# One pair ahead, one product later: reordering projections, splits and output weights in a two-block transformer kernel

## The chip, the cores and the metric
The kernel runs on one core of a Trainium2 chip. The metric is the device time of one execution in microseconds; the time before is the median of three runs.

## The reference
Two blocks of two layers each act on 256 latent tokens x and 256 context tokens (D = 1024, float32). Every layer adds a modulated mixer and a modulated squared-ReLU MLP to the residual.

```
mod   = silu(c) @ w_mod + b_mod                  # 6 x 1024 per layer and stream
a     = rms_norm(h) * g * (1 + scale) + shift
block 1 (l = 0, 1):  p, u, vs, q, k, v, gates = split(a @ w_in)
   attn  = softmax(rope(q) rope(k)^T / 8 + rpb, and q k_ctx^T) @ (v, v_ctx)      # 8 heads of 64
   y     = sig(g0)*(pool(p) @ w_po) + sig(g1)*(sgu(u, vs) @ w_so) + sig(g2)*(attn @ w_ao)
   h    += g1 * (y @ w_o);   h += g2 * (relu(a2 @ w_ff1)**2 @ w_ff2)
block 2, first layer:  mLSTM in chunks, both directions; out = rms(h) * sigmoid(o) @ w_out
block 2, second layer: sliding-window attention, 16 q heads, 4 k/v heads, window 128, a sink per head
```
In l=1 of block 1 and in the last layer the context stream is needed only for k and v.

## The kernel before
Activations stand with features on the 128 partitions and tokens along the free axis: 512 columns, context first (columns 0 to 255), then latent. A float32 product is made of three fast ones: each weight tile is split into a high half whi (ACT) and a low half wlo (VectorE, or GpSimd where `wlow` says so), each activation into xh and xl, and TensorE runs wh·xh, wh·xl and wl·xh for each of 8 k tiles. One output tile of 512 columns is thus 24 matmuls in one PSUM bank. Weights come by DMA into 3 `raw` slots, 512 KB each, and there are 3 slots each for whi and wlo. Products rotate over three PSUM banks (mm, mm, mx); scores have 2 banks (S), transposes 2 (T), outputs of the attention and small sums 1 (acc).

`gemm` takes a list of weights, loads each (`wload`), runs its matmuls (`group`) and calls an `evac` function that empties the bank. An evac may return a further part; it is kept in `late` and run by `flush` after the matmuls of the next product. `head=3` runs the first three tiles side by side, interleaved by k tile with a skew of 2; `tail=3` does the last three stream by stream while the next norm is made. `ready` is a list of weights that are loaded before their product is called; `gemm` and `gemm_rows` take weights from it before they load their own. `drip` issues pieces of the modulation products of later layers (`mod_units`: VectorE, ACT and GpSimd multiply and add, then `mod_out` transposes) at a rate for each stage. `rope` is a permutation matmul on TensorE, a multiplication on GpSimd and a multiplication and addition on VectorE; `put_q` and `put_k` split into halves for two heads. A scheduler orders the instructions of each engine ahead of time, by program order with a bonus for evacuations (`sooner`); at run time each engine works through its own list.

In block 1 (`block1`, run for l = 0 and 1) come the k products, the v product by token rows (`gemm_rows`), all four q products, then four pairs of heads of attention, then the gates and the branch products (`evac_a` adds the branches and splits them into `ys`), then the output product over wo. In the mLSTM `gates_out` runs eight gate products, after which the merged heads are split into ys for mwout. In the sliding-window layer (SWA) q is projected one pair of heads ahead already.

Of the kernel before, what the change touches and what calls it, by code (L numbers as in the profile page):

```python
# [62 lines left out]
class Builder:  # L63
# [140 lines left out]
    def gemm(self, aps, xs, c0, evac, head=0, tail=0, order=(LAT, CTX), pre=None, mid=None, flush=True):  # L204
# [7 lines left out]
        while i < n - tail:  # L212
            m = max(head, 1) if i == 0 else 1
            cols = by_stream if m > 1 and not self.ready else [(c0, T)]
            tiles = [(i + j, self.ready.pop(0) if self.ready else self.wload(aps[i + j], kt))
                     for j in range(m)]
# [7 lines left out]
            if m == 1:  # L224
                self.drip()
# [201 lines left out]
    def mod_units(self, i, groups):  # L427
# [5 lines left out]
        def unit(cg, half, k):  # L433
# [47 lines left out]
    def need(self, i, cg):  # L481
# [314 lines left out]
def block1(b, ph, l, xs, pre, after):  # L796
# [209 lines left out]
def block2_mlstm(b, ph, xs, pre, after):  # L1006
# [115 lines left out]
    def project(hf):  # L1122
# [124 lines left out]
    go = gates_out()  # L1247
    ys = b.new_xs("A")
    for hd in range(8):
        pt = b.ps("S")  # L1250
        for c in range(4):
            b.tr(pt[:, c * P:(c + 1) * P], hs[hd // 4][c][:, hd % 4, :])
        t = b.t("E")
        b.stt(t, go[hd], 1.0, pt, ALU.add, ALU.mult)
        b.act(ys[hd][0], t, scale=hn[:, hd:hd + 1])
        b.stt(ys[hd][1], t, hn[:, hd:hd + 1], ys[hd][0].bitcast(F32), ALU.mult, ALU.subtract)
# [9 lines left out]
def block2_swa(b, ph, xs, pre):  # L1266
# [12 lines left out]
    def evac_k(j, ps, a, e):  # L1279
        if a < L:  # L1280
            b.put_k(kh[2 * j:2 * j + 2], kl[j], slice(0, L), ps[:, :L - a])
        if e > L:
            t, k = b.T1(), b.T1()
            b.act(t, ps[:, max(L - a, 0):])

            def rest():
# [251 lines left out]
```

## Time and profile before
| what | value |
|---|---|
| median of 3 runs | 2288.17 us (2285.65 to 2294.4) |
| profiled execution | 2289.41 us |
| its span, first to last instruction | 2287.6 us |
| TensorE busy | 2184.0 us, 95% |
| VectorE, ACT, GpSimd busy | 1623.2, 1147.6, 703.2 us |
| mean granted clock of TensorE | 0.983 |

Times in the rows below are microseconds from the start of the span, durations too unless marked ns. PEclk is the granted clock as a share of 2.4 GHz. A stretch at 0.5 runs at 1.2 GHz, and its matmuls count as busy. Idle time of an engine stands in brackets in a row of the timeline, with the instruction that ended it.

### The profile page before, as it was taken

Reading aid. Unit: us, or ns where it says so; the run is one execution under the profiler, and the core shown is the slowest. Engines: PE = TensorE matmul, PEld = TensorE weight load, DVE = VectorE, ACT = ScalarE, POOL = GpSimd, SP = SyncE. Lnnn points to the kernel's source line nnn. Section 1 sums busy time; section 2 is a strip of 40 time slices with the busy share of each in tenths; the row PEclk is TensorE's granted clock in tenths of the full one; section 3 lists DMA queues with packets and bytes.
Section 4 is the critical chain, followed back from the end, with each engine's and each line's share of the span. In section 5 each row is a group of like instructions: output and inputs, shape, how many; then the busy total and the mean of one; then the engine's idle time right before and its main releaser. Section 6 shows DMA issues by size and latency. Waiting matters only on the chain.

```text
span 2287.6 us, 36316 instructions
## 1 busy us (share of the span) xinstructions
PE 2184.0 (95%) x13402; PEld 1851.8 (81%) x13402; DVE 1623.2 (71%) x2762; ACT 1147.6 (50%) x2122; POOL 703.2 (31%) x566
## 2 busy tenths in 40 slices
PE   6999999999999999998999899999999999898998
PEld 3777777887777787898899877778777778878998
DVE  4877656687666875778877766778876566698766
ACT  3556434454443455655545646655443433675453
POOL 2640435424221543045300524253432222423001
PEclk9999999999999999999999999999999999999999
DMA  7451445446555443367554323344555532214552
GB/s 276 133 159 59 156 130 180 138 130 187 187 188 167 146 147 107 122 206 219 184 185 158 105 80 102 115 155 130 166 190 179 170 120 74 74 47 147 190 186 96
DMA packets 128146, 336.79 MB, mean 147 GB/s; under 512 B 14944, under 2 KB 24160, under 8 KB 127968
## 3 DMA queue, kind: packets, MB, share of 16 engines
q1 hardware_dynamic: 127968, 334.46, 45.1%
q8 instruction: 106, 1.74, 0.3%
q14 instruction: 72, 0.59, 0.1%
HBM read 333.36 MB, written 1.05 MB: 146 GB/s over the span
## 4 chain that ended last, share of the span: by engine, by line
PE 44%; DVE 7%; issue 3%; ACT 2%; POOL 1%; DMA 1%; DVEq 0%; POOLq 0%; ACTq 0%; SPq 0%
PE mm L122 27%; PE mx L122 11%; PE S L122 2%; DVE wlo L130 1%; PE pv L122 1%; PE T L122 1%; PE T L126 1%; PE num L122 1%; DVE macc L119 1%; ACT whi L116 1%; DMA mraw<-wmod_in 1%; DVE A L119 1%; POOL macc L449 1%; DVE T L119 0%; POOL sums L509 0%
## 5 line engine op out<-in xcount | busy, mean ns | idle before, releaser
L122 PE MATMUL mm<-A,whi 128*128 128x256 f32 (+1 forms) x2600 | 664.6, 343 | 17.7 <-ACT A L116 7.7
L449 POOL TENSOR_TENSOR macc<-macc,mraw 128x512 f32<-128x512 f32 x244 | 364.3, 1493 | 668.9 <-ACT mraw L116 659.9
L122 PEld LDWEIGHTS mm<-A,whi 128*128 128x128 f32 x2600 | 447.4, 191 | 86.2 <-issue 15.2
L122 PE MATMUL mm<-B,whi 128*128 128x256 f32 (+1 forms) x1884 | 457.8, 333 | 6.9 <-DVE B L119 3.8
L122 PE MATMUL mm<-A,wlo 128*128 128x256 f32 (+1 forms) x1300 | 442.0, 340 | 2.6 <-DVE wlo L130 2.6
L130 DVE TENSOR_TENSOR wlo<-raw,whi 128x1024 fp32r<-128x1024 f32 x252 | 345.3, 1372 | 135.3 <-ACT whi L116 133.9
L116 ACT ACTIVATE whi<-raw 128x1024 fp32r<-128x1024 f32 x273 | 287.6, 1056 | 274.5 <-PE mm L122 167.2
L122 PEld LDWEIGHTS mm<-B,whi 128*128 128x128 f32 x1884 | 320.7, 191 | 47.3 <-DVE B L119 4.3
L116 ACT ACTIVATE mraw<-mraw,silu 128x512 f32<-128x512 f32 x244 | 175.3, 722 | 294.5 <-DVE macc L119 180.2
L122 PE MATMUL mx<-A,whi 128*128 128x512 f32 (+1 forms) x1256 | 320.0, 342 | 1.6 <-ACT G L116 1.1
L122 PE MATMUL mm<-B,wlo 128*128 128x256 f32 (+1 forms) x942 | 312.0, 332 | 2.9 <-DVE wlo L130 1.6
L119 DVE SCALAR_TENSOR_TENSOR macc<-mraw,silu,macc 128x512 f32<-128x512 f32 x244 | 258.8, 1061 | 54.9 <-DMA mraw<-wmod_in 52.5
L122 PEld LDWEIGHTS mm<-A,wlo 128*128 128x128 f32 x1300 | 248.6, 191 | 30.3 <-DVE wlo L130 3.0
L116 ACT ACTIVATE whi<-Y 128x1024 fp32r<-128x1024 f32 x152 | 160.7, 1057 | 218.3 <-PE mm L122 154.1
L130 DVE TENSOR_TENSOR wlo<-Y,whi 128x1024 fp32r<-128x1024 f32 x148 | 192.2, 1298 | 90.7 <-ACT whi L116 90.6
L122 PEld LDWEIGHTS mx<-A,whi 128*128 128x128 f32 x1256 | 216.0, 190 | 31.1 <-issue 1.3
L122 PE MATMUL mx<-A,wlo 128*128 128x512 f32 (+1 forms) x628 | 214.9, 342 | 0.3 <-DVE wlo L130 0.3
L122 PE MATMUL mx<-B,whi 128*128 128x256 f32 (+1 forms) x836 | 201.2, 329 | 6.0 <-ACT B L116 3.1
L122 PEld LDWEIGHTS mm<-B,wlo 128*128 128x128 f32 x942 | 179.8, 191 | 21.6 <-DVE wlo L130 1.8
L509 POOL TENSOR_TENSOR sums<-sums,T 128x256 f32<-128x256 f32 x84 | 91.2, 1095 | 298.7 <-ACT T L116 297.2
L119 DVE SCALAR_TENSOR_TENSOR h<-mm,mod,h 128x256 f32<-128x256 f32 x278 | 125.8, 478 | 70.6 <-PE mm L122 70.4
L122 PEld LDWEIGHTS mx<-B,whi 128*128 128x128 f32 x836 | 141.1, 191 | 23.0 <-ACT B L116 3.8
(316 smaller groups left out, 3071.3 us busy)
## 6 DMA issues: line engine op xcount, KB each, us to landing
mraw<-wmod_in SPq DMA_DIRECT2D x352, 256.0 KB, 2.9
Y<-ff_in SPq DMA_DIRECT2D x152, 512.0 KB, 3.7
raw<-ff_in SPq DMA_DIRECT2D x104, 512.0 KB, 3.5
raw<-win_in SPq DMA_DIRECT2D x68, 512.0 KB, 3.8
raw<-mwin_in SPq DMA_DIRECT2D x17, 512.0 KB, 3.5
raw<-wo_in SPq DMA_DIRECT2D x16, 512.0 KB, 4.1
raw<-swin_in SPq DMA_DIRECT2D x10, 512.0 KB, 3.5
B<-wfirst_in SPq DMA_DIRECT2D x16, 256.0 KB, 5.4
```

What stands on the lines that cost most here:

```text
L116: return self.nc.scalar.activation(out, in_, func, **kw)
L119: return self.nc.vector.scalar_tensor_tensor(out, a, scalar, b, op0, op1)
L122: return self.nc.tensor.matmul(out, lhsT=lhsT, rhs=rhs, start=start, stop=stop, **kw)
L126: return self.nc.tensor.transpose(out, in_, self.ident[:k, :k])
L130: (eng or self.nc.vector).tensor_sub(lo, src, hi.bitcast(F32))
L449: self.nc.gpsimd.tensor_add(a1, a1, raw)
L509: (adder or self.nc.gpsimd).tensor_add(sums, sums, sq)
```

## The change
q of block 1 is projected one pair ahead of its attention instead of four pairs at once; its rope and splits, those of k and those of the SWA's q and k become deferred parts, after one copy of the bank; mod_out's transposes are deferred by one more flush; evac_a adds on VectorE for the last two tiles; the last product in front of wo or mwout makes two output weights ready, and the output product begins with three tiles side by side over all columns; `drip` is called once for each tile of a head; gates_out merges and splits each head behind the next gate product; the banks of two `gemm_rows` change their order.

```diff
-    def gemm(self, aps, xs, c0, evac, head=0, tail=0, order=(LAT, CTX), pre=None, mid=None, flush=True):
+    def gemm(self, aps, xs, c0, evac, head=0, tail=0, order=(LAT, CTX), pre=None, mid=None, flush=True,
+             ahead=(), streams=True):
...
-            cols = by_stream if m > 1 and not self.ready else [(c0, T)]
+            cols = by_stream if streams and m > 1 and not self.ready else [(c0, T)]
             tiles = [(i + j, self.ready.pop(0) if self.ready else self.wload(aps[i + j], kt))
                      for j in range(m)]
+            if i + m == n:
+                self.ready = [self.wload(ap, KT) for ap in ahead]
...
-            if m == 1:
+            for _ in range(m):
                 self.drip()
...
-            self.late.append(self.mod_out(i, (cg,), 4 * half, ps))
+            columns = self.mod_out(i, (cg,), 4 * half, ps)
+            self.late.append(lambda: self.late.append(columns))
...
     def evac_k(j, ps, a, e):
-        t = b.T1()
-        b.act(t, ps[:, L:])
-        b.put_k(kh[j], kl[j], slice(0, L), ps[:, :L])
+        t = b.t("E")
+        b.act(t, ps)
         def rest():
             k = b.T1()
-            b.rope(k, t, b.perm1, b.rope1)
+            b.rope(k, t[:, L:], b.perm1, b.rope1)
+            b.put_k(kh[j], kl[j], slice(0, L), t[:, :L])
             b.put_k(kh[j], kl[j], slice(L, T), k)
         return rest
     def evac_q(j, ps, a, e):
-        q, t, k = b.t("Y", (P, 2, T), F32R), b.T1(), b.T1()
-        b.act(t, ps[:, L - a:], scale=0.125)
-        if c0 == 0:
-            b.put_q(q, slice(0, L), ps[:, :L], 0.125)
-        b.rope(k, t, b.perm1, b.rope1)
-        b.put_q(q, slice(L, T), k)
+        q, t = b.t("Y", (P, 2, T), F32R), b.t("W")
+        b.act(t[:, a:], ps, scale=0.125)
         qs.append(q)
+        def rest():
+            k = b.T1()
+            b.rope(k, t[:, L:], b.perm1, b.rope1)
+            if c0 == 0:
+                b.put_q(q, slice(0, L), t[:, :L])
+            b.put_q(q, slice(L, T), k)
+        return rest
...
-    b.gemm([win[6 + j] for j in range(4)], xs, c0, evac_q)
+    def project(j):
+        b.gemm([win[6 + j]], xs, c0, evac_q, flush=False)
+    project(0)
     for j in range(4):
+        if j < 3:
+            project(j + 1)
...
             b.weigh(o, qt, pts, vt, vcols)
+            b.flush()
...
-            nc.gpsimd.tensor_add(t, t, y[d][:, c0:])
+            (nc.vector if d > 5 else nc.gpsimd).tensor_add(t, t, y[d][:, c0:])
...
-        b.gemm2([io[f"wao{l}"][d2]], at, c0, evac_a)
+        b.gemm2([io[f"wao{l}"][d2]], at, c0, evac_a,
+                ahead=[io[f"wo{l}"][d] for d in range(2)] if d2 == 3 else ())
...
-        b.gemm(aps, ys, c0, b.add_to_h(g1), tail=3, mid=b.norm(xs, LAT, A, S))
+        b.gemm(aps, ys, c0, b.add_to_h(g1), head=3, streams=False, tail=3,
+               mid=b.norm(xs, LAT, A, S))
...
-        b.gemm_rows([io["mwv"][hf, j] for j in range(4)], T, xs, ("mm", "mm", "S", "S"),
+        b.gemm_rows([io["mwv"][hf, j] for j in range(4)], T, xs, ("S", "S", "mm", "mm"),
...
-    def gates_out():
-        go = [b.t("B") for _ in range(8)]
-        b.gemm([win[16 + j] for j in range(8)], xs, 0,
-               lambda j, ps, a, e: b.act(go[j][:, a:e], ps, AF.Tanh, scale=0.5))
-        return go
+    def gates_out(hs):
+        ys = b.new_xs("A")
+        def evac(hd, ps, a, e):
+            go = b.t("B")
+            b.act(go, ps, AF.Tanh, scale=0.5)
+            def rest():
...
+            return rest
+        b.gemm([win[16 + j] for j in range(8)], xs, 0, evac,
+               ahead=[io["mwout"][d] for d in range(2)])
+        return ys
...
-    def query(ps):
-        t, q = b.T1(), b.T1()
+    def query(_, ps, a, e):
+        t, out = b.T1(), b.t("Q", (P, 2, L), F32R)
         b.act(t, ps, scale=0.125)
-        b.rope(q, t, perm2, rope2)
-        out = b.t("Q", (P, 2, L), F32R)
-        b.put_q(out, slice(0, L), q)
-        return out
+        qs.append(out)
+        def rest():
+            q = b.T1()
+            b.rope(q, t, perm2, rope2)
+            b.put_q(out, slice(0, L), q)
+        return rest
-    b.gemm_rows([io["swv"][j] for j in range(2)], L, xs, ("mm", "mm", "mx", "S"),
+    b.gemm_rows([io["swv"][j] for j in range(2)], L, xs, ("S", "S", "mm", "mm"),
```

In the instruction lists, the numbers behind a name tell one buffer from another, and what an instruction waits for stands in brackets. First TensorE at the start of the output product of l=0, before: B_632 and B_633 are the halves of the last tile of ys, whi_734 the first wo weight.
```order
L122 MATMUL mx_736_3513<-B_630_2948,whi_734_3509 128x512 [waits Activation_49]
L122 MATMUL mx_736_3513<-B_631_2949,whi_734_3509 128x512 [waits DVE_49]
L122 MATMUL mx_736_3513<-B_630_2948,wlo_735_3510 128x512
L122 MATMUL mx_736_3513<-B_632_2950,whi_734_3509 128x512 [waits Activation_49]
L122 MATMUL mx_736_3513<-B_633_2951,whi_734_3509 128x512 [waits DVE_49]
```
These are the 19th to 23rd of the first tile's 24 matmuls. The same place after, where mm_743 and mm_744 are the second and third tile:
```order
L122 MATMUL mm_743_3526<-B_626_2944,whi_717_3451 128x512
L122 MATMUL mm_743_3526<-B_627_2945,whi_717_3451 128x512
L122 MATMUL mm_743_3526<-B_626_2944,wlo_718_3452 128x512
L122 MATMUL mm_744_3527<-B_622_2940,whi_740_3521 128x512
L122 MATMUL mm_744_3527<-B_623_2941,whi_740_3521 128x512
L122 MATMUL mm_744_3527<-B_622_2940,wlo_741_3522 128x512
L122 MATMUL mx_742_3525<-B_632_2950,whi_714_3445 128x512 [waits Activation_49]
```
The last split is read behind parts of two other tiles: 45 matmuls of the output product stand ahead of it instead of 21.

Second, TensorE in l=1 of block 1 at the products over wvs1 (tiles S), before:
```order
L122 MATMUL mm_1504_7538<-A_1424_7210,whi_1483_7476 128x256
L122 MATMUL mm_1504_7538<-A_1423_7209,wlo_1484_7477 128x256
L122 MATMUL S_1505_7566<-whi_1486_7482,A_1409_7195 128x256 [waits Activation_49]
L122 MATMUL S_1505_7566<-wlo_1487_7483,A_1409_7195 128x256 [waits DVE_49]
L122 MATMUL S_1505_7566<-whi_1486_7482,A_1410_7196 128x256
```
and after, where whi_1517 and wlo_1518 are halves of a further load of wvs1, and mx_1541 is the first k product:
```order
L122 MATMUL mm_1513_7581<-A_1433_7253,whi_1492_7519 128x256
L122 MATMUL mm_1513_7581<-A_1432_7252,wlo_1493_7520 128x256
L122 MATMUL S_1514_7609<-whi_1517_7613,A_1418_7238 128x256 [waits Activation_49]
L122 MATMUL S_1515_7610<-whi_1517_7613,A_1418_7238 128x256
L122 MATMUL mx_1541_7703<-A_1418_7238,whi_1539_7699 128x512 [waits Activation_49]
L122 MATMUL mx_1541_7703<-A_1419_7239,whi_1539_7699 128x512 [waits DVE_49]
L122 MATMUL S_1514_7609<-wlo_1518_7614,A_1418_7238 128x256 [waits DVE_49]
```
Before, the low half wlo_1487 is made on VectorE ahead of the operations T1 and A of the norm; after, wlo_1518 stands behind these:
```order
L130 TENSOR_TENSOR wlo_1496_7526<-raw_1494_7523,whi_1495_7525 128x1024 [waits DMAHW0_49,PE_49,Activation_49]
L130 TENSOR_TENSOR wlo_1499_7532<-raw_1497_7529,whi_1498_7531 128x1024 [waits DMAHW1_49,PE_49,Activation_49]
L119 SCALAR_TENSOR_TENSOR T1_1505_7549<-h_82,A1_0_7236,T1_1504_7547 128x256 [waits Activation_49]
L119 SCALAR_TENSOR_TENSOR T1_1506_7553<-h_82,A1_0_7236,T1_1504_7547 128x256 [waits Pool_49]
...
L119 SCALAR_TENSOR_TENSOR T1_1512_7577<-h_82,A1_0_7236,T1_1504_7547 128x256
L130 TENSOR_TENSOR wlo_1518_7614<-raw_1516_7611,whi_1517_7613 128x1024 [waits DMAHW3_49]
```
No product reads wlo_1496 and wlo_1499, the first pair of low halves of wvs1; between the rows of T1 stand four more of them and five that write A.

Third, VectorE in the SWA attention, before, from the low halves of the next pair's q (Q_3797) to the reduction of its scores (S_3838):
```order
L119 SCALAR_TENSOR_TENSOR Q_3797_19465<-T1_3793_19456,Q_3797_19465 64x256 [waits Activation_49] x2
L130 TENSOR_TENSOR A_3762_19320<-pv_3763_19321,A_3761_19319 128x256 [waits Activation_49]
L748 TENSOR_TENSOR sm_3809_19498<-sm_3809_19498 128x1 [waits Activation_49]
L743 TENSOR_SCALAR sm_3815_19529<-sm_3815_19529,sink_3688_18894 128x1 [waits DVE_49]
L749 RECIPROCAL sm_3809_19498<-sm_3809_19498 128x1 [waits DVE_49]
...
L750 TENSOR_SCALAR E_3817_19534<-E_3817_19534,sm_3816_19530 128x512 [waits DVE_49,PE_49]
L737 TENSOR_REDUCE sm_3840_19630<-S_3838_19624 128x1 [waits PE_49]
```
and after, for the pair with Q_3764 and S_3805 (T_3781 is its permuted q):
```order
L701 TENSOR_TENSOR T1_3783_19380<-T_3781_19377,rope2_3691_18900 128x256 [waits PE_49]
L757 RECIPROCAL sm_3787_19395<-sm_3787_19395 128x1 [waits DVE_49]
L702 TENSOR_TENSOR T1_3780_19376<-T1_3782_19379,T1_3783_19380 128x256 [waits DVE_49,Pool_49]
L758 TENSOR_SCALAR E_3788_19399<-E_3788_19399,sm_3787_19395 128x512 [waits DVE_49]
L119 SCALAR_TENSOR_TENSOR Q_3764_19321<-T1_3780_19376,Q_3764_19321 64x256 [waits Activation_49] x2
L756 TENSOR_TENSOR sm_3792_19413<-sm_3792_19413 128x1 [waits Activation_49]
L757 RECIPROCAL sm_3792_19413<-sm_3792_19413 128x1 [waits DVE_49]
L758 TENSOR_SCALAR E_3793_19417<-E_3793_19417,sm_3792_19413 128x512 [waits DVE_49]
L745 TENSOR_REDUCE sm_3807_19483<-S_3805_19477 128x1 [waits PE_49]
```
Twelve operations stood between the two before, three stand there now.

## Rows read from the trace of the kernel before

**Rows 1.** Head of the page: busy us (share of span) xinstructions
```profile
span 2287.6 us, 36316 instructions
...
PE 2184.0 (95%) x13402; PEld 1851.8 (81%) x13402; DVE 1623.2 (71%) x2762; ACT 1147.6 (50%) x2122; POOL 703.2 (31%) x566
```
**Rows 2.** Table by stretch: us, busy by engine, PEclk, DMA share, GB/s
```profile
100.00:116.00 16.00, 14.00 (x74) 10.43 (x73) 13.23 (x23) 12.73 (x28) 9.06 (x6) 1.00 0.38 122
147.00:165.00 18.00, 15.62 (x60) 11.95 (x59) 16.17 (x23) 9.59 (x18) 10.38 (x7) 0.91 0.52 171
395.00:412.00 17.00, 13.86 (x47) 10.47 (x46) 8.67 (x11) 6.74 (x11) 6.57 (x5) 0.80 0.46 140
842.00:860.00 18.00, 15.34 (x77) 12.63 (x77) 17.03 (x33) 9.73 (x18) 8.46 (x11) 0.91 0.65 221
880.00:892.00 12.00, 7.87 (x28) 5.73 (x27) 6.94 (x12) 7.39 (x16) 1.29 (x1) 0.86 0.17 49
1323.00:1340.00 17.00, 14.16 (x53) 10.70 (x52) 9.68 (x22) 6.85 (x11) 0.00 (x0) 0.90 0.32 104
1500.00:1520.00 20.00, 17.91 (x90) 13.59 (x89) 18.53 (x27) 11.29 (x17) 7.75 (x6) 1.00 0.38 123
1952.00:1965.00 13.00, 11.60 (x96) 11.25 (x95) 4.42 (x9) 9.68 (x22) 4.75 (x2) 1.00 0.23 78
1971.00:1985.00 14.00, 10.14 (x59) 8.79 (x58) 9.18 (x23) 7.28 (x17) 7.67 (x6) 0.88 0.31 104
1985.00:2070.00 85.00, 81.74 (x641) 66.67 (x641) 74.28 (x251) 61.56 (x154) 18.27 (x11) 1.00 0.18 57
...
1559.00:1580.00 21.00, 19.69 (x163) 18.78 (x155) 20.78 (x40) 13.18 (x30) 5.84 (x5) 1.00 0.27 89
```
**Rows 3.** Timeline of PE, 395 to 413: start, us, what, [idle before <-releaser]
```profile
400.80 1.52 PE L122 MATMUL mx<-B,whi 128*128 128x512 f32 x2 [3.14 <-ACT B L116]
...
410.22 0.62 PE L122 MATMUL mm<-B,whi 128*128 128x512 f32 x2
```
**Rows 4.** Timeline of POOL, 385 to 402
```profile
393.19 1.73 POOL L986 TENSOR_TENSOR G<-G,Y 128x512 f32<-128x512 f32 x1 [1.23 <-DVE G L119]
...
397.84 2.24 POOL L986 TENSOR_TENSOR G<-G,Y 128x512 f32<-128x512 f32 x1
```
**Rows 5.** Timeline of DVE, 832 to 853
```profile
840.92 3.33 DVE L119 SCALAR_TENSOR_TENSOR T<-h,A,T 128x256 f32<-128x256 f32 x3
...
849.38 1.22 DVE L130 TENSOR_TENSOR wlo<-raw,whi 128x1024 fp32r<-128x1024 f32 x1
```
**Rows 6.** Timeline of PE, 876 to 895
```profile
885.35 0.76 PE L122 MATMUL mx<-whi,A 128*128 128x512 f32 x1 [3.24 <-DVE B L719]
```
**Rows 7.** Timeline of ACT, 1324 to 1331
```profile
1327.16 0.63 ACT L116 ACTIVATE nM<-W 64x512 fp32r<-64x512 f32 x1 [2.90 <-DVE W L1068]
1327.70 0.57 ACT L116 ACTIVATE Q<-mm 128x512 f32<-128x512 f32 x1
```
**Rows 8.** Timeline of PE, 838 to 856
```profile
850.49 0.50 PE L122 MATMUL mm<-A,whi 128*128 128x512 f32 x1 [1.58 <-ACT whi L116]
```
**Rows 9.** Timeline of DVE, 1990 to 1997
```profile
1991.46 0.42 DVE L693 TENSOR_TENSOR T<-T,rope 128x256 f32<-128x256 f32 x1
1991.80 1.01 DVE L748 TENSOR_TENSOR sm<-sm 128x1 f32<-128x1 f32 x1
...
1992.86 0.41 DVE L694 TENSOR_TENSOR T<-T,T 128x256 f32<-128x256 f32 x1
1993.19 0.15 DVE L749 RECIPROCAL sm<-sm 128x1 f32<-128x1 f32 x1
...
1993.59 0.47 DVE L750 TENSOR_SCALAR E<-E,sm 128x512 f32<-128x512 f32 x1
...
1994.55 0.87 DVE L119 SCALAR_TENSOR_TENSOR Q<-T,Q 64x256 fp32r<-64x256 f32 x2
```
**Rows 10.** Timeline of POOL, 1985 to 2000
```profile
1990.42 2.37 POOL L130 TENSOR_TENSOR wlo<-raw,whi 128x1024 fp32r<-128x1024 f32 x1 [6.05 <-ACT whi L116]
```

More of the change, by code (lines that the diff above doesn't have):

```diff
@@ L245, in last_tiles, with gemm2 @@
             steps.finish()
-    def gemm2(self, aps, xs, c0, evac, tail=0, mid=None):
+    def gemm2(self, aps, xs, c0, evac, tail=0, mid=None, ahead=()):
         n = len(aps)
@@ L251, in gemm2 @@
             w = self.wload(aps[i], 8)
+            if i + 1 == n:
+                self.ready = [self.wload(ap, KT) for ap in ahead]
             for j in range(2):
@@ L484, in need @@
             self.one()
-        self.flush()
+        while self.late:
+            self.flush()
     def scales(self, i, which):
@@ L1001, in block1 @@
         R = []
-        b.gemm(aps, ys, c0, b.add_to_h(g1, then=scale), tail=3)
+        b.gemm(aps, ys, c0, b.add_to_h(g1, then=scale), head=3, streams=False, tail=3)
         b.mlp(l, xs, c0, "B", pre=b.norm(xs, LAT, A, S, R), plain=(rs, R), **after)
@@ L1235, in heads @@
         return hs
-    def gates_out():
-        go = [b.t("B") for _ in range(8)]
-        b.gemm([win[16 + j] for j in range(8)], xs, 0,
-               lambda j, ps, a, e: b.act(go[j][:, a:e], ps, AF.Tanh, scale=0.5))
-        return go
+    def gates_out(hs):
[4 more added lines that the diff above has]
+            def rest():
+                pt = b.ps("S")
+                for c in range(4):
+                    b.tr(pt[:, c * P:(c + 1) * P], hs[hd // 4][c][:, hd % 4, :])
+                t = b.t("E")
+                b.stt(t, go, 1.0, pt, ALU.add, ALU.mult)
+                b.act(ys[hd][0], t, scale=hn[:, hd:hd + 1])
+                b.stt(ys[hd][1], t, hn[:, hd:hd + 1], ys[hd][0].bitcast(F32),
+                      ALU.mult, ALU.subtract)
+            return rest
+        b.gemm([win[16 + j] for j in range(8)], xs, 0, evac,
+               ahead=[io["mwout"][d] for d in range(2)])
+        return ys
     prj = project(0)
@@ L1246, in block2_mlstm @@
     hs.append(heads(1, prj[0], prj[1], prj[3], states(1, prj[2], prj[3])))
[L1247 to L1256, printed above, removed]
+    ys = gates_out(hs)
     b.banks = cycle(["mm", "mm", "mx"])
@@ L1260, in block2_mlstm @@
     xs = b.new_xs("B")
-    b.gemm([io["mwout"][d] for d in range(8)], ys, 0, b.add_to_h(b.mod[i][:, 2]), tail=3,
+    b.gemm([io["mwout"][d] for d in range(8)], ys, 0, b.add_to_h(b.mod[i][:, 2]), head=3,
+           streams=False, tail=3,
            mid=b.norm(xs, LAT, A, S))
@@ L1279, in evac_k, with rest @@
     def evac_k(j, ps, a, e):
[L1280 to L1286, printed above, removed]
+        t = b.T1()
+        b.act(t, ps)
+        def rest():
+            k = t
+            if a == L:
+                k = b.T1()
                 b.rope(k, t, perm2, rope2)
-                b.put_k(kh[2 * j:2 * j + 2], kl[j], slice(L, T), k)
-            return rest
-    def query(ps):
-        t, q = b.T1(), b.T1()
+            b.put_k(kh[2 * j:2 * j + 2], kl[j], slice(a, e), k)
+        return rest
+    def query(_, ps, a, e):
+        t, out = b.T1(), b.t("Q", (P, 2, L), F32R)
         b.act(t, ps, scale=0.125)
-        b.rope(q, t, perm2, rope2)
-        out = b.t("Q", (P, 2, L), F32R)
-        b.put_q(out, slice(0, L), q)
-        return out
+        qs.append(out)
+        def rest():
+            q = b.T1()
+            b.rope(q, t, perm2, rope2)
+            b.put_q(out, slice(0, L), q)
+        return rest
     b.gemm([win[8 + j] for j in range(2)], xs, 0, evac_k, head=2, pre=pre, flush=False)
-    b.gemm_rows([io["swv"][j] for j in range(2)], L, xs, ("mm", "mm", "mx", "S"),
+    b.gemm_rows([io["swv"][j] for j in range(2)], L, xs, ("S", "S", "mm", "mm"),
                 lambda c, ps: b.act(vt[c], ps))
@@ L1305, in project @@
     def project(t):
-        b.gemm([win[t]], xs, L, lambda _, ps, a, e: qs.append(query(ps)))
+        b.gemm([win[t]], xs, L, query, flush=False)
     b.wlow = nc.gpsimd
@@ L1323, in block2_swa @@
             b.weigh(o, qt, pts, vt, vcols)
+            b.flush()
         b.pair_out(o, a, L)
```

## The prediction, made blind
> **What bounds the kernel now.** I read the head of the page first: TensorE is busy 2184.0 of 2287.6 us [rows 1], so the time can only fall where it idles or runs at its lower clock. Then I went through its timeline for idle time with a releaser, and put every place that the change touches into one table by stretch [rows 2]. A stretch's loss has two parts: its length less PE busy, and its length times (1 - PEclk), since a matmul at half clock counts as busy. From 395 to 412 that is 17.00 - 13.86 = 3.14 us idle and 17 x 0.20 = 3.4 us of clock, 6.5 us together. The single rows agree: a gap of 3.14 us behind ACT's split, then two matmuls in 1.52 us where the same two take 0.62 later [rows 3]. So a stall of two or three microseconds here costs about twice itself; the granted clock falls from 2.4 to 1.2 GHz behind it.
>
> The same arithmetic on the other touched stretches gives 100 to 116: 2.0; 147 to 165: 2.4 + 1.6 = 4.0; 880 to 892: 4.1 + 1.7 = 5.8; 1323 to 1340: 2.8 + 1.7 = 4.5; 1500 to 1520: 2.1; 1952 to 1965: 1.4; 1971 to 1985: 3.9 + 1.7 = 5.5. Those eight hold 31.9 us, which is the ceiling of what the change can take away. Three stretches may lose: 842 to 860 (now 4.3), 1985 to 2070 (3.3 of 85) and 1559 to 1580 (VectorE busy 20.78 of 21).
>
> **The change part by part: what goes.**
> The wo product (395 to 412): the last split of ys is read by the 22nd matmul before and by the 46th after, because three tiles go side by side, and their first two weights are made earlier. At 0.23 us a matmul (0.62 for two that overlap by 0.16) [rows 3] that is 5.5 us later, against a gap of 3.14. The adds of evac_a that fed it took 1.73 and 2.24 us on GpSimd [rows 4]; the slack is over 2 us even if they take as long on VectorE, so I take all 6.5. Late next is the third weight's low half, which is now queued on VectorE just ahead of the last split; the same slack covers its 1.2 us (the last row there) [rows 5].
>
> The k products (880 to 892): the wait of 3.24 us ended on put_k's last subtraction, which still read the bank [rows 6]. One 128x512 copy on ACT takes 0.57 us [rows 7] and then the bank is free. Gap and clock go; 0.8 is kept back for the later rope, so 5.0.
>
> The v product of the mLSTM (1323 to 1340): the bank's evacuation stood on ACT behind nM, which waited for VectorE (nM at 1327.16, the evacuation right behind it at 1327.70) [rows 7]. With the banks in the other order it comes first on ACT. All 4.5.
>
> mod_out's transpose one flush later (100 to 116): 2.0 becomes 0.2 (the transpose now has 24 matmuls ahead of it), 1.8 gained. The swv banks (1952 to 1965): 1.4, since no split stands between bank and copy now.
>
> q's rope in block 1 (147 to 165): the wait on ACT goes, but q0's scores now follow its rope with only half a product (2.8 us) between; I take 3.0 of 4.0. The start of the SWA attention (1971 to 1985): its first wait goes with the second product ahead, its second one (an exp) does not depend on the change; half, 2.8 of 5.5. gates_out (1500 to 1520): the merge is spread over the gate products, but ys shares its buffers with the products' input, so that no part of it can be written before the last product; 1.2 of 2.1. The l=1 wo and the added SWA copies I cost at nothing: ACT is busy 61.56 of 85 us there.
> Sum: 6.5 + 5.0 + 4.5 + 1.8 + 1.4 + 3.0 + 2.8 + 1.2 = 26.2 us.
>
> **What comes.**
> First, weights loaded twice. In l=1 the list b.ready holds win1, wvs0 and wvs1; the product over win1 takes the first, and the new line that fills b.ready from an empty "ahead" throws the other two away. gemm_rows then loads both again: two DMAs of 512 KB, two ACT copies and two VectorE subtractions. The price is not these but their place: the new low half stands behind 13 VectorE operations (eight T1, five A) that start at 840.92 and take some 0.4 to 0.5 us each with ACT between them, so to about 847.8, then 1.22 us [rows 5] to 849.0. TensorE waits for it there, runs the remaining 46 matmuls of wvs in 46 x 0.12 = 5.5 us (256 columns, half of the 0.23 above) to 854.5, and only then the k product that began in earnest after its wait at 850.5 [rows 8]: some 3.7 us later, and up to 1.7 more of low clock after the longer idle time. Bounds: 2 (if the low half gets in early) and 8 (if the second DMA lands late); I take 5.0.
>
> Second, the rope of q one pair ahead. Before, twelve VectorE operations stood between the low halves of the next pair's q and the reduction of its scores; now there are two short ones and a normalization. In the SWA attention the chain on VectorE behind the permutation is 0.42 + 0.15 + 0.41, a normalization of 0.47, and 0.87 for the low halves, 2.3 us [rows 9]; with ACT's halves between, near 2.8. TensorE has left for that time seven matmuls of 0.12, seven pv and four transposes, about 18 x 0.12 = 2.2 us. So 0.6 us a pair, 7 pairs, 4.2. Lower bound 0 (the scores may find their own bank late anyway); upper bound from the same chain in before, which took from 1991.46 to 1994.55 + 0.87 = 1995.42, 4.0 us [rows 9]: 1.8 a pair, 13. I take 4.2, near the bare chain, since only one operation there is far over its usual length. In block 1 the same holds for 3 pairs in each layer, where the next q product is cover that can be placed freely: 0.3 a pair, 2.0; bounds 0 and 11, the same 1.8 a pair.
> The exception is the row at 1991.80: an addition on 128x1 took 1.01 us, while GpSimd ran a 2.37 us subtraction from 1990.42 [rows 9, 10]. The Trainium skill (SBUF — State Buffer, "SBUF: two separate sides") says that VectorE's operations with two SBUF inputs and GpSimd's reads share a port pair, and that whichever starts first holds it for its whole instruction. The trace agrees here: 1.01 us against 0.15 for a like-sized reciprocal. By that rule the move of evac_a's adds is worth more than its own difference, and a rope chain that meets the 2.37 us row is longer by up to that; it speaks for the slower case below.
>
> Third, drip() runs three times behind a head of three: about five modulation units come forward into 425 to 470 and 1559 to 1580, where VectorE has 0.2 us left. They fill idle slots in program order; 0.5, from 0 to 4.
>
> Sum of costs: 5.0 + 4.2 + 2.0 + 0.5 = 11.7. Net 26.2 - 11.7 = 14.5 us. The profiled execution took 2289.41 us, so 2274.9; the median of the three runs is 1.24 lower, which gives 2273.7. I say 2273.
>
> **The rivals.**
> 1. The waits change their place. For it: each of the eight gaps was the last wait of a chain with others close behind (two waits in 1971 to 1985, several in 1500 to 1520), and the engines around them stay as loaded. If half of the 26.2 comes back as new waits, the net is 13.1 - 11.7 = 1.4: about 2287. Against it: in 395 to 412, 880 to 892 and 1323 to 1340 the next event is well ahead.
> 2. Slower: the q chain comes onto the path in all attention stages. Place: the first scores of each pair, 7 in the SWA, 3 in each layer of block 1. Price: 1.8 us by the measured chain, and a gap of that size is followed by low clock (1.7 us in 1971 to 1985), of which I count half: 2.65 x 13 = 34.5 in place of 6.2. Then 26.2 - 5.0 - 0.5 - 34.5 = -13.8: 2289.41 + 13.8 - 1.24, about 2302. It turns slower than before from 1.6 us a pair, and by over 0.5% from 2.5. For it: TensorE and VectorE are both near full there (81.74 and 74.28 of 85), and the 1.01 us row. Against it: the bare chain, and that block 1 has whole q products as filler.
> 3. Better: the pairs cost nothing, and the second load of wvs is mostly hidden because the k product's own low half was late in before too (849.38) [rows 5]. 26.2 + 3 more from the half-counted stretches, less 2.5: about 2261.
> 4. The change doesn't do what it says: the weights made ahead and the deferred splits stay where the buffers let them, and only the double load is felt: about 2288.
>
> **How the numbers follow.** Chances: forecast 0.50, rival 1 0.22, rival 2 0.09, rival 3 0.15, rival 4 0.04. Within 0.5% is 11.4 us, about what a measurement of this kernel can tell from no change: 2276.7 to 2299.6. The forecast's own range is 2265 to 2281, nine tenths of it under 2276.7: faster 0.45 + 0.15 = 0.60; within 0.05 + 0.22 + 0.04 = 0.31; slower 0.09. The range leaves out rival 2 and the outer part of rival 3: 2259 to 2289.
>
> **What would show it.** Right: no wait over 0.5 us at the first tile of wo in l=0, at the second pair of k products in l=1 and at the mLSTM's v product, and granted clock 1.0 around each; a new wait of some 8 us on the low half of wvs1, with wvs1 read four times in all; scores of SWA pairs that wait some 0.5 us on VectorE. Wrong: waits over 2 us at each pair's scores (rival 2), new waits of 1 to 3 us a few products behind the old ones (rival 1), or no long wait at wvs1 (rival 3).

## The result, and the profile after
The changed kernel takes 2309.59 us (median of 4 runs, 2308.47 to 2310.49), the kernel before 2291.28 beside it (4 runs): the ratio is 1.008 with a 95% interval of 1.0063 to 1.0097, slower by 0.8%. The forecast was 2273, its range ended at 2289, and "slower" had 0.09.

The head of the page after:
```profile
span 2308.4 us, 36273 instructions
...
PE 2193.7 (95%) x13402; PEld 1860.2 (81%) x13402; DVE 1634.0 (71%) x2768; ACT 1153.7 (50%) x2126; POOL 678.8 (29%) x562
```
The engines do almost the same work as in [rows 1], and TensorE runs the same 13402 matmuls. The 20.8 us more of span are waits (11.1 us more idle time) and the low clock behind them (9.7 us more busy time for the same matmuls). The table by stretch says where, columns as in [rows 2]:
```profile
395.00:412.00 17.00, 16.43 (x84) 12.67 (x83) 11.28 (x16) 7.82 (x12) 5.76 (x5) 1.00 0.48 156
842.00:860.00 18.00, 9.64 (x54) 8.60 (x55) 17.49 (x28) 7.67 (x14) 8.26 (x10) 0.72 0.63 222
872.00:892.00 20.00, 20.00 (x88) 16.29 (x87) 16.25 (x28) 16.96 (x37) 6.41 (x6) 1.00 0.35 115
905.00:980.00 75.00, 67.94 (x507) 57.17 (x505) 49.54 (x138) 40.64 (x84) 6.06 (x6) 0.95 0.35 112
1310.00:1346.00 36.00, 34.44 (x191) 29.04 (x191) 32.48 (x52) 25.05 (x52) 14.77 (x17) 1.00 0.35 114
2094.00:2125.00 31.00, 21.45 (x121) 20.88 (x120) 22.70 (x36) 12.72 (x28) 11.37 (x7) 0.68 0.51 170
```
The aimed-at stretches at 395 (wo), 872 to 892 (the k products of l=1) and 1310 to 1346 (the mLSTM's v) have their full clock now, and the k products have no idle time at all. But the head of wvs1 (842) is idle for 8.4 of 18 us, the attention of l=1 (905 to 980) for 7.1 of 75, and the MLP head of the last layer (2094 to 2125), which the diff does not touch, for 9.6 of 31 at a clock of 0.68. Of these two the table of before has:
```profile
905.00:980.00 75.00, 72.89 (x581) 63.01 (x581) 56.14 (x146) 47.15 (x94) 10.84 (x9) 1.00 0.39 125
...
2088.00:2119.00 31.00, 25.99 (x200) 25.24 (x200) 25.21 (x37) 17.58 (x36) 14.38 (x6) 0.94 0.53 184
```
The longest waits stand in the timeline of PE after, each with its releaser:
```profile
848.64 1.22 PE L122 MATMUL mx<-A,whi 128*128 128x512 f32 x2 [6.29 <-ACT whi L116]
851.93 0.58 PE L122 MATMUL S<-wlo,A 128*128 128x256 f32 x1 [2.07 <-DVE wlo L130]
...
932.45 1.22 PE L122 MATMUL S<-Q,Y 128*128 128x512 f32 x2 [4.08 <-ACT E L116]
...
947.13 0.73 PE L122 MATMUL S<-Q,Y 128*128 128x512 f32 x2 [1.70 <-ACT E L116]
...
1110.17 0.77 PE L122 MATMUL mm<-A,whi 128*128 128x256 f32 x2 [6.91 <-DVE T L667]
...
1452.45 0.49 PE L122 MATMUL num<-Y,W 128*128 128x129 f32 x2 [1.49 <-ACT B L116]
...
1985.69 1.65 PE L122 MATMUL S<-Q,Q 128*128 128x512 f32 x3 [3.23 <-DVE Q L119]
...
2119.59 0.76 PE L122 MATMUL mm<-B,whi 128*128 128x256 f32 x2 [6.86 <-DVE T L667]
```
The releasers name the double load (848, 851), the exps of l=1 (932, 947), the emptying of banks in MLP heads (1110, 2119), a copy in the mLSTM (1452), and a q half in the SWA (1985). The MLP heads had waits before, too, but shorter ones. PE before, at the same two heads:
```profile
1097.36 0.76 PE L122 MATMUL mm<-A,whi 128*128 128x256 f32 x2 [4.26 <-DVE T L659]
...
2103.39 0.44 PE L122 MATMUL mm<-B,whi 128*128 128x256 f32 x1 [3.37 <-DVE B L119]
```

To place all of the time I compared, at the same amount of matmul work done (columns streamed), how far a profiled run lags behind before. The change of that lag over a stretch of before's time is what the stretch lost (plus) or won. Single profiled runs differ from the medians by some us. In the table, "forecast" is what the prediction's terms give for a stretch, "after" is the changed kernel, and g2 is the fastest version below. 1610 to 1930, where every run is some 0.5 us behind, is left out.

| stretch | what stands there | forecast | after | g2 |
|---|---|---|---|---|
| 0–130 | mod_out, start | -1.8 | -0.1 | +0.9 |
| 130–380 | attention, l=0 | -2.0 | +1.0 | +0.8 |
| 380–430 | wo, l=0 | -6.5 | -5.6 | -5.5 |
| 430–835 | rest of l=0 | +0.3 | +3.4 | -0.5 |
| 835–900 | wvs1 and k, l=1 | 0 | +1.5 | -2.1 |
| 900–1045 | attention, l=1 | +1.0 | +9.7 | -0.7 |
| 1045–1130 | MLP head, l=1 | 0 | +2.6 | +0.9 |
| 1130–1310 | MLP, l=1, and on | 0 | -1.3 | +4.3 |
| 1310–1345 | mLSTM v | -4.5 | -4.6 | -5.0 |
| 1345–1480 | mLSTM heads | 0 | +5.3 | -0.9 |
| 1480–1610 | gates, mwout | -1.0 | -2.2 | -1.7 |
| 1930–1968 | swv | -1.4 | -1.0 | -1.0 |
| 1968–2075 | SWA attention | +1.4 | +3.5 | +1.2 |
| 2075–2130 | MLP head, SWA layer | 0 | +6.8 | -1.3 |
| 2130–end | | 0 | +1.7 | 0 |
| all | | -14.5 | +20.9 | -10.0 |

### The profile page after: what moved, and what is told of

It reads as the page before. It is cut to its first block, busy times and chain, and to the rows that moved or that the text cites. A ratio compares the mean times of both kernels' runs of the same rounds, so it can differ in the third digit from the quotient of the medians.

```text
span 2308.4 us, 36273 instructions
## 1 busy us (share of the span) xinstructions
PE 2193.7 (95%) x13402; PEld 1860.2 (81%) x13402; DVE 1634.0 (71%) x2768; ACT 1153.7 (50%) x2126; POOL 678.8 (29%) x562
## 3 DMA queue, kind: packets, MB, share of 16 engines
HBM read 334.40 MB, written 1.05 MB: 145 GB/s over the span
## 5 line engine op out<-in xcount | busy, mean ns | idle before, releaser
L455 POOL TENSOR_TENSOR macc<-macc,mraw 128x512 f32<-128x512 f32 x244 | 358.6, 1470 | 666.4 <-ACT mraw L116 656.5
L119 DVE SCALAR_TENSOR_TENSOR macc<-mraw,silu,macc 128x512 f32<-128x512 f32 x244 | 251.5, 1031 | 36.8 <-DMA mraw<-wmod_in 34.2
```

The lines of the kernel that those rows point to most:

```text
L119: return self.nc.vector.scalar_tensor_tensor(out, a, scalar, b, op0, op1)
L455: self.nc.gpsimd.tensor_add(a1, a1, raw)
```

## The experiments
My theory after the result had four causes: the double load; the interleaved q products of l=1; two-input VectorE operations that run beside GpSimd's low halves; and the drips that moved. The rival was the forecast's own rival 2, the q chain in all attention stages. Unless said otherwise each kernel is the changed one with one edit, and ratios are to before.

**The ready list kept (e1).**
```diff
-            if i + m == n:
+            if ahead and i + m == n:
```


> The changed kernel, but a product without weights to make ahead leaves the list of ready weights alone, so that wvs1 is loaded once. Theory (the double load costs TensorE its two waits of 6.29 and 2.07 us at 848 and 852, and low clock behind them): the stretch up to the k products of l=1 ends 5 to 7 us earlier, 2303 to 2305 us in all against 2309.6. Rival (the waits there come from the norm's chain on VectorE, and the load only hides in it): under 2 us less, about 2308.

Measured: 2301.36 (5 runs), 1.0051 [1.0034, 1.0068]. Why the second load costs its place and not its work, on VectorE after:
```profile
840.94 5.21 DVE L119 SCALAR_TENSOR_TENSOR T<-h,A,T 128x256 f32<-128x256 f32 x5
846.08 3.47 DVE L119 SCALAR_TENSOR_TENSOR A<-T,mod,A 128x256 fp32r<-128x256 f32 x5
849.47 1.27 DVE L119 SCALAR_TENSOR_TENSOR T<-h,A,T 128x256 f32<-128x256 f32 x3
850.66 1.22 DVE L130 TENSOR_TENSOR wlo<-raw,whi 128x1024 fp32r<-128x1024 f32 x1
```
The low half stands behind eight T and five A, as the forecast had it, and is done at 851.88 where that had 849.0: the first eight of these rows took 0.84 to 1.49 us each beside GpSimd's rows, not 0.4 to 0.5. In e1 the waits of 6.29 and 2.07 are gone; 1.07 and 1.57 at the k products are left, as before had them (1.08, 1.58). The stretch 835 to 900 goes from +1.5 to -2.3, but these are sums of two things. After loses 8.1 from 835 to 855, at the double load, and wins 6.1 from 880 to 890, at the k products. In e1 the first is 0, and a wait that after doesn't have takes 3.7 at 875 to 880:
```profile
877.04 1.22 PE L122 MATMUL T<-E,perm 128*128 128x256 f32 x2 [1.93 <-ACT E L116]
```
So the double load cost 8 at its place, and 4 net, since its delay covered this wait. The medians differ by 8.2; the profiled run of e1 was its slowest (2306.13), so that some 4 us of its gain are in no stretch.

**Low halves on VectorE at the MLP heads (e2, and f1: the same edit in the kernel before).**
```diff
                            [(0, L + 2)], evac_plain, steps)
-                self.wlow = self.nc.gpsimd
```


> The changed kernel, but at the head of the MLPs of l=1 and of the sliding-window layer the low halves of the weights stay on VectorE and are not handed to GpSimd. Theory (three two-input operations of the norm on VectorE that take 2.3 to 2.6 us in place of 0.47 are held up by GpSimd's subtractions of 2.4 us beside them, and the emptying of the product's banks is queued behind): these rows go back to 0.47, the waits of 6.91 and 6.86 us at 1110 and 2120 fall to 3 or less, 8 to 12 us less in all, about 2299. Rival (VectorE is simply full there; the low halves it now makes itself, 1.2 us each, cost what the blocked rows did): the waits stay at 5 to 7 us and the time at 2307 to 2311.

> The kernel before with one edit: at the head of the MLPs of l=1 and of the sliding-window layer the low halves of the weights stay on VectorE. Theory (GpSimd's subtractions hold up the norm's two-input operations there, in before too: 2.61 and 2.56 us in place of 0.47 at 1091 to 1094): the gaps of 4.26 us at 1097 and 3.37 us at 2103 go, 5 to 9 us less with the clock, about 2283. Rival (the gain of 10.7 us by the same edit on the changed kernel came from its own order of the bank-emptying operations): under 3 us here, about 2289.

e2: 2298.9 (6 runs), 1.004 [1.0022, 1.0058]. f1: 2286.26 (10 runs), 0.9985 [0.9972, 0.9997]. VectorE after, ahead of the 6.86 us wait:
```profile
2111.43 2.31 DVE L119 SCALAR_TENSOR_TENSOR B<-T,mod,B 128x256 fp32r<-128x256 f32 x1 [0.30 <-ACT B L116]
2113.67 2.56 DVE L119 SCALAR_TENSOR_TENSOR T<-h,A,T 128x256 f32<-128x256 f32 x1
2116.16 2.55 DVE L119 SCALAR_TENSOR_TENSOR B<-T,mod,B 128x256 fp32r<-128x256 f32 x1
2118.63 0.47 DVE L119 SCALAR_TENSOR_TENSOR T<-h,A,T 128x256 f32<-128x256 f32 x1
2119.03 0.41 DVE L667 TENSOR_TENSOR T<-mm,T 128x256 f32<-128x256 f32 x1
```
and GpSimd in the same time:
```profile
2111.07 4.87 POOL L130 TENSOR_TENSOR wlo<-raw,whi 128x1024 fp32r<-128x1024 f32 x2 [6.10 <-ACT whi L116]
2115.91 2.52 POOL L130 TENSOR_TENSOR wlo<-Y,whi 128x1024 fp32r<-128x1024 f32 x1
```
Three subtractions on GpSimd, three stretched rows on VectorE, each ending within 0.3 us of the end of one of them; the next of the same form takes 0.47. The first row that empties a bank, L667, is queued behind all three. VectorE before, where the line is L659:
```profile
2095.75 0.42 DVE L659 TENSOR_TENSOR T<-mm,T 128x256 f32<-128x256 f32 x1
2096.34 1.99 DVE L119 SCALAR_TENSOR_TENSOR B<-T,mod,B 128x256 fp32r<-128x256 f32 x1 [0.17 <-ACT B L116]
2098.25 2.60 DVE L643 TENSOR_TENSOR Q<-Q 128x256 f32<-128x256 f32 x1
2100.78 2.55 DVE L119 SCALAR_TENSOR_TENSOR B<-T,mod,B 128x256 fp32r<-128x256 f32 x1
```
Before had three slow rows, too, but one bank was emptied ahead of them, and its longest wait there was 3.37. The change rearranged that list without touching its code. Which part of it did so, other runs tell: in e3, where the modulation's extra pieces are taken out, the wait of 6.91 at the head of l=1 is back at before's 4.26 (at 1095.59) and 1045 to 1130 goes from +2.6 to -8.1, while the wait of 6.86 stays; in f2, with the old q of the SWA, the wait of 6.86 falls to 3.35, while that of l=1 stays. In e2 the waits are 0.94 (of 6.86) and 0.83 (of 6.91); on VectorE:
```profile
2111.31 0.47 DVE L119 SCALAR_TENSOR_TENSOR T<-h,A,T 128x256 f32<-128x256 f32 x1
2111.71 0.41 DVE L667 TENSOR_TENSOR T<-mm,T 128x256 f32<-128x256 f32 x1
```
The two stretches give back 6.9 and 8.5 us, but the SWA loses 4.4 more: there an operation on VectorE now starts with a low half on GpSimd. VectorE, then GpSimd, of e2:
```profile
1995.09 2.67 DVE L757 TENSOR_SCALAR E<-E,sm 128x512 f32<-128x512 f32 x1
```
```profile
1995.14 2.35 POOL L130 TENSOR_TENSOR wlo<-raw,whi 128x1024 fp32r<-128x1024 f32 x1 [1.21 <-ACT whi L116]
```
TensorE waits 2.23 us for it. In before the edit is worth 0.15%, about 3.4 us (interval 0.7 to 6.4), against 10.7 in the changed kernel, so most of what e2 wins is harm that came with the new order.

**q of block 1 (e4: all four products together, their ropes still deferred; g3: the pair's flush moved behind both heads).**
```diff
-    project(0)
+    b.gemm([win[6 + j] for j in range(4)], xs, c0, evac_q)
     for j in range(4):
-        if j < 3:
-            project(j + 1)
```


> The changed kernel, but all four q products of block 1 come before the attention as in the kernel before, with their rope and splits still deferred. Theory (in l=1 the rope of the next pair stands on ACT and VectorE in front of the current pair's softmax, and costs waits of 4.08 and 1.70 us at 932 and 947 with low clock behind): the stretch of the l=1 attention is back to its old length, 6 to 8 us less, about 2302.5, and no wait over 1 us remains at the scores there. Rival (the waits come from the weights' splits that share ACT and VectorE with the attention): they stay, 2307 to 2311.

e4: 2306.99 (4 runs), 1.0076 [1.0048, 1.0104]. The attention of l=1 (905 to 980) goes from +7.3 to 0.0; l=0 gets worse (130 to 380 from +1.0 to +3.9), which I had not expected. TensorE there, and ACT before it:
```profile
169.72 1.22 PE L122 MATMUL T<-W,perm 128*128 128x256 f32 x2 [6.49 <-ACT W L116]
```
```profile
167.52 0.72 ACT L116 ACTIVATE mraw<-mraw,silu 128x512 f32<-128x512 f32 x1 [2.73 <-issue]
...
169.09 0.58 ACT L116 ACTIVATE W<-mm 128x512 f32<-128x512 f32 x1
```
The permutation of the last q waits for its copy W, which stands on ACT behind a row of the modulation and the high half of a weight; that row itself starts after 2.73 us of idle time for which the profile names no releaser, so why ACT is late is not shown. So e4 is not a plain undoing, and only its l=1 half is read. Its median is 2.6 us under the changed kernel, which is within the noise of the two.
```diff
             b.weigh(o, qt, pts, vt, vcols)
-            b.flush()
+        b.flush()
```


> The changed kernel with one line moved: in block 1 the deferred rope and splits of the next pair's q are issued behind the second half of the current pair's attention, not between its halves. Theory (between the halves they stand on ACT and VectorE ahead of the second half's softmax, and the scores wait for its exp): the waits of 4.08 and 1.70 us at 932 and 947 go or fall under 1, and 905 to 980 is 5 to 7 us shorter; the next pair's first scores may wait 1 to 2 us instead; 2304 in all. Rival (the exp waits for the splits of the gates' weights, not for the rope): the waits stay, 2308 to 2311.

g3: 2305.38 (5 runs), 1.0049 [1.0031, 1.0066]. The 4.08 is gone, a wait of 1.70 stands at 934.88, and a new 1.38 came at 959.06. ACT after, ahead of the 4.08:
```profile
927.24 0.86 ACT L116 ACTIVATE Y<-T 64x256 fp32r<-64x256 f32 x2 [1.40 <-DVE T L702]
928.62 1.06 ACT L116 ACTIVATE whi<-raw 128x1024 fp32r<-128x1024 f32 x1 [0.52 <-ACT Y L116]
931.62 0.69 ACT L116 ACTIVATE E<-S,sm 128x512 f32<-128x512 f32 x1 [1.94 <-DVE sm L749]
```
and VectorE:
```profile
927.70 0.87 DVE L119 SCALAR_TENSOR_TENSOR Y<-T,Y 64x256 fp32r<-64x256 f32 x2 [0.48 <-ACT Y L116]
929.71 1.23 DVE L130 TENSOR_TENSOR wlo<-raw,whi 128x1024 fp32r<-128x1024 f32 x1 [1.15 <-ACT whi L116]
930.85 0.48 DVE L746 CUSTOM_DVE_ANT_0 S<-S,T,sm 128x256 f32<-128x256 f32 x1
```
The exp waits for the score row S, which stands behind the next pair's q halves and the low half of a weight. ACT of g3, ahead of the 1.70:
```profile
933.10 1.06 ACT L116 ACTIVATE whi<-raw 128x1024 fp32r<-128x1024 f32 x1 [1.89 <-PE mx L122]
934.06 0.67 ACT L116 ACTIVATE E<-S,sm 128x512 f32<-128x512 f32 x1
```
Here no rope stands between; a weight's high half alone stands ahead of the exp. So the 4.08 needs the deferred rope between the two heads, and the 1.70 comes from the weight splits of the interleaved products. Moving the rope does not cure the stage: 905 to 980 goes only from +7.3 to +6.0, with the 1.70 and the 1.38 and two waits of 0.75 in place of the 4.08. Rope and splits both go with the interleaving, and e4 and f3, which have none in l=1, are at 0.0.

**Drips (e3: none behind a head of three).**
```diff
-            for _ in range(m):
+            if m == 1:
                 self.drip()
```


> The changed kernel, but pieces of the modulation are issued once behind a head of several tiles only where a head has one tile, as in the kernel before. Theory (the early pieces shift all later ones, so that GpSimd's additions now fall beside the mLSTM's two-input operations on VectorE, which take 1.05 and 1.57 us in place of 0.16 at 1449 and 1450): the 4.8 us lost in the second half of the mLSTM heads come back, 4 to 6 us less, about 2304.5. Rival (the stretch lost its time to the other bank order or to gates_out): no change there, 2308 to 2311.

e3: 2312.21 (4 runs), 1.0096 [1.0073, 1.0119]. My total failed. 1440 to 1480 came back (+4.8 to +0.6), and so did the head of the MLP in l=1 (above), but the units that were not placed there pressed later: 1345 to 1440 cost 9.6 and 1480 to 1610 went from -2.2 to +9.6, with waits of 3.33 (a kv product at 1423.98) and 4.16 (macc at 1571.14). What the early units do in the mLSTM, VectorE after:
```profile
1448.93 1.05 DVE L119 SCALAR_TENSOR_TENSOR sm<-sm 128x2 f32<-128x2 f32 x1
...
1450.09 1.57 DVE L119 SCALAR_TENSOR_TENSOR sm<-sm 128x2 f32<-128x2 f32 x1
```
and GpSimd:
```profile
1448.20 1.76 POOL L455 TENSOR_TENSOR macc<-macc,mraw 128x512 f32<-128x512 f32 x1 [1.33 <-DVE W L1223]
...
1450.39 1.26 POOL L455 TENSOR_TENSOR macc<-macc,mraw 128x512 f32<-128x512 f32 x1
```
An operation on 256 numbers takes 1.05 and 1.57 us while GpSimd adds for the modulation. In g2 it stands free of GpSimd:
```profile
1439.78 0.16 DVE L119 SCALAR_TENSOR_TENSOR sm<-sm 128x2 f32<-128x2 f32 x1
```

**The SWA (f2: q as in before; f5: the first four low halves left on VectorE).** f2's edit is that of the diff shown above for `query`, backwards, without the flush in the pair.


> The changed kernel with the sliding-window layer's q as before: rope and splits directly behind each product, no flush inside the pair. Theory as predicted (0.6 us a pair for the shorter lead): the SWA attention is 4 us shorter, and the small waits on VectorE at the pairs' first scores go. Rival (only the start of the attention is late, by the one wait of 3.23 us at 1986 on VectorE): the pairs take as long as before, and 0 to 3 us come back at the start alone; 2307 to 2310.

f2: 2298.74 (6 runs), 1.0029 [1.0014, 1.0044]. The attention goes from +3.5 to -0.2 (from 1990 to 2075 alone, +4.2 to 0.0), and the MLP head behind it from +6.8 to +1.7, since its list falls back to before's order (a wait of 3.35 at 2115.00, as the 3.37 of before). I had expected 4 us and got 10.9: of the 8.8 that the two stretches show, the larger half was in code that neither edit touches. The theory had the place wrong, too: after its first wait of 3.23, no pair's scores wait for VectorE in the changed kernel. Its waits stand at transposes behind a normalization (0.3 to 0.4 us, once 1.5) and behind the last pair (0.75 and 0.47).
```diff
-    b.wlow = nc.gpsimd
     project(0)
     for t in range(8):
+        if t == 3:
+            b.wlow = nc.gpsimd
```


> The changed kernel, but in the sliding-window layer the low halves of the first four q weights are made on VectorE, and GpSimd takes over from the fifth. Theory (the first rope's addition on VectorE took 2.54 us in place of 0.41 at 1982 because GpSimd was inside a subtraction of 2.4 us, and its multiplication stood behind four of them in GpSimd's queue): the addition is back under 0.5 us and the wait of 3.23 us at 1986 falls under 1.5; 3 to 5 us less with the clock, about 2305.5. Rival (the rope's chain itself is what lasts): the wait stays over 2.5 us, 2308 to 2311.

f5: 2303.43 (4 runs), 1.0044 [1.0029, 1.0059]. VectorE after, then VectorE of f5:
```profile
1982.19 2.54 DVE L702 TENSOR_TENSOR T<-T,T 128x256 f32<-128x256 f32 x1 [1.17 <-POOL T L700]
1985.22 0.87 DVE L119 SCALAR_TENSOR_TENSOR Q<-T,Q 64x256 fp32r<-64x256 f32 x2 [0.48 <-ACT Q L116]
```
```profile
1978.65 0.43 DVE L702 TENSOR_TENSOR T<-T,T 128x256 f32<-128x256 f32 x1
1979.56 2.89 DVE L119 SCALAR_TENSOR_TENSOR Q<-T,Q 64x256 fp32r<-64x256 f32 x2 [0.49 <-ACT Q L116]
```
Ahead of the low half on GpSimd the rope's addition is short again and the wait of 3.23 falls to 1.64 (under 1.5 was expected); what is left is the next row, which met the next low half (2.59 us on GpSimd from 1978.71).

**The causes together (f3: e1, e2, and q one pair ahead in l=0 only).**
```diff
+    if l == 0:
+        project(0)
+    else:
+        b.gemm([win[6 + j] for j in range(4)], xs, c0, evac_q)
...
-        if j < 3:
+        if l == 0 and j < 3:
```


> The changed kernel with three of the earlier edits together: ready weights kept (wvs1 loaded once), the low halves at the heads of the two MLPs on VectorE, and q one pair ahead in l=0 only. Theory (the three losses are separate): the gains add, 4 to 7, 11 and 7 us: 2309.6 - 23 = 2286.5, a little under the kernel before. Rival (each edit moves the pieces of the modulation and makes a new collision elsewhere): under half of the sum, 2297 or more.

f3: 2288.69 (10 runs), 0.9989 [0.9978, 1.0]. That is 20.9 us under the changed kernel, about what e1, e2 and e4 gave by their medians (8.2 + 10.7 + 2.6), though e4 has a loss in l=0 that f3 has not. It is level with before.

**Faster than both (g2: f3, f2, and several drips only behind output products; g4: the same with gates_out as before, weights still ahead).**
```diff
-            for _ in range(m):
+            for _ in range(m if m == 1 or not streams else 0):
```


> The mixed kernel (ready weights kept, low halves on VectorE at the two MLP heads, q ahead in l=0 only), and beside it the sliding-window q as before, and pieces of the modulation issued once per tile where an output product begins with three, but not behind the heads of the MLPs. Theory (the extra pieces behind the MLP heads are what moved into the second half of the mLSTM; behind the output products they only replace what one tile after another issued before): the 4.9 us lost there come back, the SWA attention gives 4: 2288.7 - 9 = 2280, under both kernels. Rival (moving the pieces again makes a collision elsewhere, as it did when they were dripped once per head): 2286 to 2292.

> The same as the mixed kernel with the old drips and the old sliding-window q, and the mLSTM's merge of heads again behind all eight gate products (two weights of the output product still ready ahead). Theory (the buffers of ys are those of the gate products' input, so that the merge waits for the last product and nothing is won by spreading it): 0 to 2 us less around the output product, 2279. Rival (the spread merge is what shortens 1545 to 1610 by 3.5 us): 2 to 4 us more, 2283.

g2: 2276.19 (6 runs), 0.9928 [0.9912, 0.9944]. g4: 2277.86 (4 runs), 0.993 [0.991, 0.9949]. g2 is 0.7% faster than before and 33.4 us under the changed kernel. Its mLSTM heads are back at -0.9 and 430 to 835 at -0.5. In f3 they stand at +6.8 and +3.1, in f2 at +5.7 and +4.4, so neither of these two did it: the drips had cost there. g4 equals g2 within the noise: spreading the merge won nothing that the medians show (in the profiled runs 1480 to 1610 is 3.1 longer without it).

## Why the prediction was wrong
The kernel was forecast 14.5 us faster and lagged 20.9 in the profiled run, 35.4 apart. By the table, the attention of l=1 makes 8.7 of that, the two MLP heads 9.4, the two stretches of the drips (430 to 835, 1345 to 1480) 8.4, the attention of l=0 3.0, the SWA attention 2.1, and wvs1 with the k products 1.5.

**Right.** The losses named in [rows 2] were real, and where the next event was well ahead the gain came nearly whole: wo in l=0 -5.6 (forecast 6.5), the mLSTM's v -4.6 (4.5), the swv banks -1.0 (1.4), mod_out -1.8 in 70 to 130 (1.8; a run-to-run difference in the first 70 us hides it in the table), the k products -6.1 (5.0). The double load was seen and its mechanism held. The SWA pairs cost 4.2, as forecast, and f2 takes just this back; but the waits are not at the pairs' first scores, where the forecast had them, so the number is partly luck.

**The step that failed in most places: the extra pressure was priced only where the diff moves instructions.** 1045 to 1130 and 2075 to 2130 stood at 0 and lost 2.6 and 6.8. The rule of the Trainium skill (SBUF — State Buffer, "SBUF: two separate sides") was weighed for one row of the SWA. The trace agrees with it in four more places: 0.47 against 2.31 to 2.56, 0.41 against 2.54, 0.16 against 1.05 and 1.57. The forecast kept it as a note to the slower case instead of asking of every VectorE list, in every stage, what would stand behind a stretched row. e2 and f5 show it by taking the GpSimd work away, e3 and f2 that the drips and the SWA's q moved the two lists.

**q of block 1: "0.3 a pair, 2.0" for both layers.** In l=1 alone it was 7.3, the largest single miss. The cover, a whole q product, brings its own work: its weight splits stand on ACT and VectorE ahead of the exp, as the rope does. The bound of 11 held it; the value near the bare chain was wrong. Rival 2 was right on the side of before on which the kernel fell, and close on the size in this stage (2.65 a pair, 8.0 for three); it was wrong on the SWA. In l=0 the gain of 3.0 did not show (+1.0 for -2.0): the wait of 2.16 at 150.83 went, and the first scores now wait 1.59 at 152.17 for a half of q on VectorE, and exps cost 0.97 and 0.58 behind it. That is the first pair's chain, which the forecast gave 1.0 of its 4.0.

**The double load: 5.0, bounds 2 and 8.** It cost 8.1 at its place. The forecast gave each T and A 0.4 to 0.5 us, though three T in its own row took 3.33 [rows 5]; beside GpSimd they took 0.84 to 1.49. The term was mis-sized, not the mechanism. With the load taken away the stretch gains only 2.3, since a wait at 877 on the deferred chain (a permutation that waits for ACT's copy E) then replaces part of the old 3.24 [rows 6]; this is rival 1, in e1, f3, g2 and g4 but not in the changed kernel.

**The drips: 0.5, bound 4.** 1345 to 1480 alone lost 5.3, and 430 to 835 lost 3.4; g2 gives both back. They do fill idle slots, but at 1449 the slots are those beside short two-input rows. That this is how they cost elsewhere is not shown.

**The start of the SWA: -2.8.** It gained 0.7 (1968 to 1990). The waits of [rows 2] went; the rope's addition behind a low half on GpSimd put 3.23 in their place. In f5 the start gains 2.4.

**Open.** Why g2 gains 12.5 us over f3 in the medians but only 7.1 in the profiled runs; why it loses 4.3 from 1130 to 1310; how much of 430 to 835 belongs to which drip; and the value of the new q order in l=0 by itself, since e4 made another wait there.

## What to carry to other kernels
With a static order, compare every engine's list in the stages behind the edit too, and look there for the instruction that empties a bank: what moves in front of it can cost more than the edit's own work. A product used as cover brings its weight splits onto the engines of the chain that it covers. State that is carried from call to call (a list of weights made ready, a drip's count) is checked at every caller for what a default argument does to it.

## What the runs showed of the hardware
A VectorE row with two operands in SBUF that starts inside a GpSimd addition or subtraction waits for that one's end and then does its own columns. In after, 58 modulation rows of 128x512 start well inside one, and all end 0.55 us behind it; 23 low halves of 128x1024 end 1.08 behind; of nine norm rows of 128x256 six end 0.28 behind, and three kept their 0.47 to 0.48. So the price is the rest of GpSimd's row, whatever the size of VectorE's: 128x2 took 1.05 us in place of 0.16. Rows that read a PSUM bank keep their time: the first row of [rows 9], which multiplies the permuted q out of its bank, took 0.42 us inside the subtraction of [rows 10], and in after 25 rows that add a product's bank to h, inside GpSimd rows, all took 0.47 to 0.49.

Operations with one large input can wait, too: TENSOR_SCALAR on 128x512, with one column as its second operand, took 2.67 us beside a low half of 2.35 (0.49 at 932.63 after).

Which of the two goes first could not always be read from the recorded starts. At 1978.65 in f5 the VectorE row started 0.06 us ahead of GpSimd's, kept its 0.43, and GpSimd's subtraction took 2.59. But the rows at 1450.09 after and at 1995.09 in e2 start in the record 0.30 and 0.05 us ahead of the GpSimd row whose end they wait for, and were stretched to 1.57 and 2.67. Times on GpSimd are rough in this profile, so the order of starts that close is not certain.
